# Latents as tokens x features from w_down to the output, the last MLP summed in PSUM, late adaLN units for latents alone, and weights split ahead

## The chip, the core and the metric

The kernel runs on one core of a Trainium2 chip. The metric is the device time of one execution in microseconds (us). In the profile the engines are PE (TensorE: PE for matmuls, PEld for the loads of their stationary operand), DVE (VectorE), ACT (ScalarE), POOL (GpSimd) and SP (SyncE, whose queue issues nearly all loads).

## The reference

256 latent tokens and 256 context tokens of 1024 features go through two layers. Layer 0 mixes tokens by a convolution, layer 1 by a bidirectional chunkwise mLSTM with 4 heads. Each mixer is followed by an MLP. The context leaves the computation within layer 1: only latents have an output.

```
sh1, sc1, g1, sh2, sc2, g2 = split(silu(c) @ ada_w[i] + ada_b[i], 6)      # per layer; c_ctx for the context
y = mixer(modulate(h, sh1, sc1))                                          # layer 1: ... @ w_down, 2048 -> 1024
h = layer_norm(ALPHA * h + g1 * y, ln1_g[i], ln1_b[i])
h = layer_norm(ALPHA * h + g2 * mlp(modulate(h, sh2, sc2)), ln2_g[i], ln2_b[i])
# mlp(u) = square(relu(u @ w1)) @ w2, 1024 -> 4096 -> 1024
# mLSTM output per head: y = (group_norm(o_f * h_f + o_b * h_b) * gn_g + skip * xc) * silu(z), then @ w_down
```

Everything is fp32. The mixer's layer 1 output of each head (512 features) is multiplied by that head's 512 rows of w_down, and the four products are summed.

## The kernel before

**Precision.** A product of two fp32 matrices is made of three fp32r matmuls: each operand is split into hi and lo, and hi·hi, hi·lo and lo·hi are summed in PSUM. `mm3` (L174 on; L177, L180, L181) has the weights as the stationary operand and up to 512 columns of tokens as the moving one, so its result is features x tokens. `mm3t` (L183; L185 to L187) has a block of 128 tokens as the stationary operand and 512 columns of weights as the moving one; its result is tokens x features. Weights come in 1 MB loads into `raw` (3 buffers, `raw_load`, L148) and are split in pieces of 1024 columns: a copy by ACT to `wh` and a subtraction by DVE to `wl` (4 buffers each, `split_w`, L160).

**Layout.** Nearly all activations lie as features x tokens. A layer norm (`Norm`, L428) over features is then a sum over partitions: PE sums columns with matmuls (`mean`, `col`), ACT squares, DVE sums the squares, and at the end (`finish`, L485) PE spreads the reciprocal roots over all partitions (L513), after which `apply` (L517) takes two DVE instructions for each of the 8 feature blocks.

**adaLN.** Layer 1 has 12 units of 512 columns of `ada_w`: 0 to 1 are sh1, 2 to 3 sc1, 4 to 5 g1, 6 to 7 sh2, 8 to 9 sc2, 10 to 11 g2. `AdaV` (L347) makes units 0 to 8 on DVE while PE works on something else: for each 128 rows one 256 KB load (`ar`), then a multiply-add each for the context and the latents into two accumulators `L`; PE sums the accumulators over partitions (L378), ACT copies, PE transposes (L387). Units 9, 10 and 11 are made by PE (`Ada`, L323, L297) inside the first norm of layer 1's end, as filling (`fill`, L1440), from six 1 MB loads.

**The end of layer 1**, where the change lies:
1. The attention stage follows the table `Z.att` (L46): main work (`o0` to `o3`: `gate_o`, output gates; then `D1 D2` and `D3`: `down`, products with w_down) and side work (`G` decay, `W` weights, `A` attend, `D0`) taken in turns.
2. `down` (L1398) makes, for each head and each of 8 feature blocks, 12 matmuls of 256 columns (`mm3`), and adds each result to the residual `hl` (features x tokens).
3. The join: the norm over `hl` with its filling, the modulation to `u` (L1456 to L1458), then the MLP.
4. `mlp` (L868) in four chunks of 1024 hidden features: 8 hidden blocks of 24 matmuls of 256 columns, their relu, square and split (`e1`), then 8 output blocks of 24 matmuls of 256 columns with w2, each added to `hl` by DVE (`e2`, L899).
5. The tail: the last norm, scale and offset by ACT (L1472), and 8 stores.

**Order.** A scheduler of the framework sets the order of instructions on each engine from its own estimates; every engine works through its queue in order. SP's queue is in order as well. PSUM has 8 banks under the tags mm (3), ln (2), cv (2) and fl (1).

## Time and profile before

| | |
|---|---|
| three runs | 1763.49, 1768.0, 1763.47 us; median 1763.49 us |
| the profiled execution | 1771.28 us, of which the span from the first to the last instruction 1769.6 us |
| matmuls | 10394 |
| DVE, ACT, POOL busy | 61%, 42%, 2% of the span |
| join: last matmul of w_down to the first of the last MLP | 1539.02 to 1562.76 us |
| last MLP, first to last matmul | 1562.76 to 1752.12 us |
| tail: end of the last MLP's matmuls to the end | 1752.12 to 1769.57 us |

Busy time is the time in which an engine has an instruction in progress. Matmuls overlap their neighbours, so the pace of a stretch is read from the count of matmuls in it, not from the length of one. Rows of groups read: line, engine, operation, output<-inputs, shapes, count | busy us, mean ns of one | idle time before it and what ended it. Rows of the timeline read: start, length (us), engine, line, operation, tiles, shapes, count, and in brackets idle time before it with what ended it.

### The profile page before, as it was taken

The numbers are of one execution on the slowest core, as the hardware profiler recorded it, in microseconds if no ns is written. First come the engines' busy times: TensorE is split into PE (matmuls) and PEld (weight loads), VectorE is DVE, ScalarE is ACT, GpSimd is POOL, SyncE is SP. The second block draws the span as 40 slices with busy tenths as digits, with TensorE's granted clock in tenths as the row PEclk, the third lists the DMA queues.
The fourth block names the chain that finished last, engine by engine and source line by source line (L and its number), as shares of the span: only waits on it lengthen the run. The fifth ranks groups of instructions, "written<-read, shape, count | busy, mean of one in ns | idle before, by whom it ended". The sixth has DMA issues, their size and how long they took to land.

```text
span 1769.6 us, 26027 instructions
## 1 busy us (share of the span) xinstructions
PE 1721.4 (97%) x10394; PEld 1452.6 (82%) x10394; DVE 1086.0 (61%) x1997; ACT 737.4 (42%) x1164; POOL 31.5 (2%) x84
## 2 busy tenths in 40 slices
PE   8999999999999999999999999999999999989996
PEld 5655798878788999976777998988777888879996
DVE  5456896566545787762234763633677766866666
ACT  3311663232324464542333433432577645434443
POOL 0000000000000000000000000000021000000000
PEclk9899999999999999999999999999999999989998
DMA  9333525344324075577745742533544555655551
GB/s 354 121 118 126 188 74 202 121 141 143 131 96 143 25 222 178 177 241 267 249 148 168 262 155 84 206 143 123 200 155 171 193 201 199 216 189 191 174 184 48
DMA packets 67817, 297.59 MB, mean 168 GB/s; under 512 B 6834, under 2 KB 22706, under 8 KB 36720
## 3 DMA queue, kind: packets, MB, share of 16 engines
q1 hardware_dynamic: 50032, 281.25, 45.3%
q10 hardware_dynamic: 17664, 14.69, 2.5%
q8 instruction: 82, 1.34, 0.3%
q14 instruction: 39, 0.32, 0.1%
HBM read 280.17 MB, written 15.73 MB: 167 GB/s over the span
## 4 chain that ended last, share of the span: by engine, by line
PE 91%; DVE 4%; ACT 2%; DMA 1%; issue 1%; SPq 0%; POOL 0%; POOLq 0%; ACTq 0%; DVEq 0%
PE mm L177 22%; PE mm L181 22%; PE mm L180 22%; PE mm L187 3%; PE mm L185 3%; PE mm L186 3%; PE fl L297 1%; DMA raw<-ada_w 1%; DVE wl L155 1%; PE cv L762 1%; PE fl L693 1%; PE ln L177 1%; PE ln L180 1%; PE ln L181 1%; PE cv L186 1%
## 5 line engine op out<-in xcount | busy, mean ns | idle before, releaser
L154 ACT CAST wh<-raw 128x1024 fp32r<-128x1024 f32 x354 | 367.9, 1048 | 606.1 <-PE mm L180 440.7
L155 DVE TENSOR_TENSOR wl<-raw,wh 128x1024 fp32r<-128x1024 f32 x354 | 431.8, 1224 | 298.7 <-ACT wh L154 296.5
L180 PE MATMUL mm<-u,wh 128*128 128x256 f32 (+1 forms) x1400 | 448.7, 321 | 0.0
L177 PE MATMUL mm<-u,wh 128*128 128x256 f32 (+1 forms) x1272 | 399.8, 315 | 7.4 <-ACT u L1456 2.1
L181 PE MATMUL mm<-u,wl 128*128 128x256 f32 (+1 forms) x1272 | 398.3, 314 | 1.1 <-DVE wl L155 1.1
L180 PEld LDWEIGHTS mm<-u,wh 128*128 128x128 f32 x1400 | 269.3, 192 | 18.9 <-DVE mv L528 0.8
L177 PEld LDWEIGHTS mm<-u,wh 128*128 128x128 f32 x1272 | 244.7, 193 | 29.9 <-ACT wh L154 7.4
L181 PEld LDWEIGHTS mm<-u,wl 128*128 128x128 f32 x1272 | 245.2, 193 | 16.7 <-DVE wl L155 2.3
L177 PE MATMUL mm<-hid,wh 128*128 128x256 f32 (+1 forms) x512 | 166.0, 324 | 0.0
L181 PE MATMUL mm<-hid,wl 128*128 128x256 f32 (+1 forms) x512 | 165.3, 323 | 0.0
L180 PE MATMUL mm<-hid,wh 128*128 128x256 f32 (+1 forms) x512 | 165.3, 323 | 0.0
L365 DVE SCALAR_TENSOR_TENSOR L<-ar,cs,L 128x512 f32<-128x512 f32 x126 | 90.0, 748 | 66.6 <-DMA ar<-ada_w 66.4
L177 PEld LDWEIGHTS mm<-hid,wh 128*128 128x128 f32 x512 | 97.4, 190 | 7.9 <-issue 0.2
L180 PEld LDWEIGHTS mm<-hid,wh 128*128 128x128 f32 x512 | 97.4, 190 | 7.7 <-issue 0.2
L181 PEld LDWEIGHTS mm<-hid,wl 128*128 128x128 f32 x512 | 97.4, 190 | 7.5
L177 PE MATMUL mm<-xm,wh 128*128 128x512 f32 x256 | 102.9, 402 | 0.0
L185 PE MATMUL mm<-wh,xl 128*128 128x512 f32 x256 | 101.0, 396 | 0.7 <-ACT wh L154 0.5
L186 PE MATMUL mm<-wh,xl 128*128 128x512 f32 x256 | 100.6, 393 | 0.6 <-DVE xl L155 0.6
L181 PE MATMUL mm<-xm,wl 128*128 128x512 f32 x256 | 100.3, 392 | 0.0
L187 PE MATMUL mm<-wl,xl 128*128 128x512 f32 x256 | 100.1, 394 | 0.2
L177 PE MATMUL mm<-qq,wh 128*128 128x272 f32 x256 | 74.1, 289 | 0.0
L181 PE MATMUL mm<-qq,wl 128*128 128x272 f32 x256 | 73.9, 289 | 0.0
(414 smaller groups left out, 2774.1 us busy)
## 6 DMA issues: line engine op xcount, KB each, us to landing
raw<-w SPq DMA_DIRECT2D x64, 1024.0 KB, 4.9
raw<-wo SPq DMA_DIRECT2D x32, 1024.0 KB, 4.9
raw<-ada_w SPq DMA_DIRECT2D x30, 1024.0 KB, 4.9
ar<-ada_w SPq DMA_DIRECT2D x72, 256.0 KB, 2.9
raw<-wv SPq DMA_DIRECT2D x16, 1024.0 KB, 6.0
raw<-wqT SPq DMA_DIRECT2D x16, 1024.0 KB, 5.3
raw<-wq SPq DMA_DIRECT2D x16, 1024.0 KB, 5.3
raw<-wk SPq DMA_DIRECT2D x16, 1024.0 KB, 4.8
```

What stands on the lines that cost most here:

```text
L154: c = nc.scalar.copy(hi, src)
L155: nc.vector.tensor_tensor(lo, src, hi.bitcast(F32), op=ALU.subtract)
L177: a = nc.tensor.matmul(ps, wh, xh, start=start, stop=False)
L180: nc.tensor.matmul(ps, wh, xl, start=False, stop=False)
L181: nc.tensor.matmul(ps, wl, xh, start=False, stop=stop)
L185: nc.tensor.matmul(ps, xh, wh, start=start, stop=False)
L186: nc.tensor.matmul(ps, xl, wh, start=False, stop=False)
L187: nc.tensor.matmul(ps, xh, wl, start=False, stop=stop)
L297: a = nc.tensor.matmul(ps[32 * j:32 * j + 32], cs[:, kt, 14 - 2 * v:46 - 2 * v], blocks[kt], start=first and kt < 4, stop=last and kt >= 4 ...
L365: nc.vector.scalar_tensor_tensor(a, w, c, a, op0=ALU.mult, op1=ALU.add)
L693: nc.tensor.matmul(wqs[0][32 * j:32 * j + 32, :], wgp[0][:, kt, :], raw[:, j * 512:(j + 1) * 512], start=kt == 0, stop=kt == ET - 1, tile_ ...
L762: return nc.tensor.matmul(o[r:r + 64, :], g_[:, r:r + 64], ps_[b][i], start=i == 0, stop=i == 1, tile_position=(0, r))
```

## The change

What it does, in the order of the program:

- **adaLN.** `AdaV` takes a list of units and of streams. Units 0 to 3 still have both streams, and four accumulators (two units) are now summed by four matmuls side by side. Units 6 to 9 (sh2, sc2) are made for latents alone, four accumulators at a time. Units 4 and 5 (g1), also for latents alone, are not brought to columns: a matmul with 128 columns of ones gives their sum on every partition as a row `G1` (two fp32 matmuls of 512 columns), to which the bias, loaded as a row on all partitions, is added. Units 10 and 11 (g2) are made by PE in the join; two matmuls (`gate2`) turn them into the row `G2`.
- **Residual.** After the up-projections' norm the latents are scaled by ACT and transposed by PE (16 transposes of 128x128) into `R`, tokens x features.
- **w_down** is laid out for `mm3t`: for each head 2 token blocks x 2 halves of 512 features, 12 matmuls of 512 columns each. Head 0 is added to `R` by DVE and POOL; heads 1 to 3 are summed in four PSUM banks (the three of mm and the one of fl). Head 3's weights are split ahead into buffers of their own (`E3`).
- **Join.** For each token block: the product with `G1`, the sum into `R` and BN_STATS on DVE, the root by ACT, two DVE instructions that normalise (512 columns each), 8 transposes on PE, and for each of the 8 feature blocks an ACT instruction (hi) and a DVE instruction, then a DVE subtraction for two blocks (lo). Two units of filling are left.
- **Last MLP.** w2 is laid out for `mm3t`; the sum over all four chunks stays in four PSUM banks (two of ln, two of cv). In the last chunk six of the eight weight pieces are held back so that token block 0 ends before block 1. While it runs POOL prepares the next residual in `R`.
- **Tail.** For each token block the norm as in the join; block 0's scale and offset by ACT and POOL, block 1's by four DVE instructions; four stores of 256 KB.
- `bo` is loaded in two parts for each head; `es` has one buffer where it had two.

The core of the diff:

```
-    att = [..., ['o3', 'A2', 1], ['D1 D2', 'A3', 1.2], ['D3', '', 0]]
+    att = [..., ['o3', 'A2', 1], ['D1 E3 D2', 'A3', 1.2], ['D3', '', 0]]
...
-    ada_g2, ada_n1, ada_n2 = Ada(0, 10, 2), AdaVs(1, 0, 4), AdaVs(1, 4, 8 - Z.fill)
+    ada_g2, ada_n1, ada_n2 = Ada(0, 10, 2), AdaV(1, range(4), (0, 1)), AdaV(1, range(6, 10), (1,), (4, 5))
...
+    R = xp.tile([P, 2, D], F32, name="res")
     for f in range(0, DT, 2):
+        t, tr = tmp("S"), psum("cv")
         for i in range(2):
+            nc.scalar.activation(t[:, i * C:(i + 1) * C], x[f + i][:, HI], AF.Identity, scale=..., bias=...)
+            for tt in range(2):
+                nc.tensor.transpose(tr[:, tt * C + i * P:...], t[:, i * C + tt * P:...], ident)
+        nc.scalar.copy(R[:, :, f * P:(f + 2) * P], tr.rearrange("p (t c) -> p t c", t=2))
...
-                for kt in range(4):
-                    mm3(ps, *kcol(w, (i % 2) * 4 + kt), *yy[h][kt], kt == 0, kt == 3)
-                nc.vector.scalar_tensor_tensor(hl[m], ps, g1[:, m:m + 1], hl[m], op0=ALU.mult, op1=ALU.add)
+        def mms(ps, ws, hf, t, first, last):
+            for kt in range(4):
+                mm3t(ps, yy[h][kt][0][:, BLK[t]], yy[h][kt][1][:, BLK[t]], *ws[hf][kt], first and kt == 0, last and kt == 3)
...
+    def residual(t, hf, ps, G):
+        e_ = tmp("E")
+        nc.vector.tensor_tensor(e_, ps, G[:, HF[hf]], op=ALU.mult)
+        nc.vector.tensor_tensor(R[:, t, HF[hf]], R[:, t, HF[hf]], e_, op=ALU.add)
+        nc.vector.bn_stats(nst[t][0][:, hf, :], R[:, t, HF[hf]])
+    def row_norm(t):
+        nc.vector.bn_aggr(mv[:, 0:2], ...)
+        nc.scalar.activation(mv[:, 2:3], mv[:, 1:2], AF.Sqrt, bias=eps)
+        nc.vector.reciprocal(mv[:, 2:3], mv[:, 2:3])
...
+    def ln1(t):
+        mv = row_norm(t)
+        for g_ in range(2):
+            nc.vector.tensor_scalar(R[:, t, HF[g_]], R[:, t, HF[g_]], mv[:, 0:1], mv[:, 2:3], op0=ALU.subtract, op1=ALU.mult)
+            tr = psum("ln")
+            for i in range(4):
+                nc.tensor.transpose(tr[:, i * P:(i + 1) * P], R[:, t, ...], ident)
+            for i in range(4):
+                nc.scalar.activation(UH[f // 2][:, f % 2, ts], tr[:, sl], AF.Identity, scale=ca[...], bias=cb[...])
+                nc.vector.tensor_scalar(y[:, sl], tr[:, sl], ca[...], cb[...], op0=ALU.mult, op1=ALU.add)
+                if i % 2:
+                    nc.vector.tensor_tensor(UL[f // 2][:, :, ts], y..., UH[f // 2].bitcast(F32)[:, :, ts], op=ALU.subtract)
...
+    for t in range(2):
+        for b_, op in ((GA, ALU.mult), (BA, ALU.add)):
+            nc.gpsimd.tensor_tensor(R[:, t, :], R[:, t, :], b_, op=op)
...
+        def w2_mm(w, kt, t, hf):
+            mm3t(acc[t][hf], hid[kt][0][:, ts], hid[kt][1][:, ts], w[0][hf], w[1][hf],
+                 c == 0 and kt == 0, c == 3 and kt == DT - 1)
```

**PE at the join.** Before, from the first filling after w_down's last matmul to the first matmuls of the last MLP: `fl<-raw,cs` is the filling, `ln<-inv_c` and `ln<-L,ones` the norm, `fl<-fold` the end of the filling, `mm<-u,wh` the MLP.

```order
L297 MATMUL fl_13941<-raw_13942,cs 32x512 x4
L297 MATMUL fl_13941<-raw_13944,cs 32x512 x4
L480 MATMUL ln_13954<-inv_c,x_11458 128x1 x2
L297 MATMUL fl_13941<-raw_13959,cs 32x512 x4
L480 MATMUL ln_13971<-inv_c,x_11459 128x1 x2
L297 MATMUL fl_13941<-raw_13961,cs 32x512 x4
L513 MATMUL ln_14006<-L_14004,ones 128x512
L297 MATMUL fl_13941<-raw_13984,cs 32x512 x4
L297 MATMUL fl_13941<-raw_13986,cs 32x512 x4
L305 MATMUL fl_13998<-fold,F_13996 128x6 x4
L177 MATMUL mm_14082<-u_14025,wh_13923 128x256
L177 MATMUL mm_14083<-u_14025,wh_13927 128x256
```

The same place now, from w_down's last matmul on: `ln<-ident,res` are the transposes (token block 0's two halves, then block 1's first half), `x_13686` the hi and `x_13690` the lo of the first two feature blocks. Block 1's second half stands 10 rows further, behind the first eight matmuls and the last filling.

```order
L186 MATMUL fl_13321<-xl_13477,og_13589 128x512
L1517 MATMUL ln_13698<-ident,res 128x128 x4
L1517 MATMUL ln_13715<-ident,res 128x128 x4
L296 MATMUL fl_13731<-raw_13732,cs 32x512 x4
L296 MATMUL fl_13731<-raw_13734,cs 32x512 x4
L296 MATMUL fl_13731<-raw_13744,cs 32x512 x4
L1517 MATMUL ln_13762<-ident,res 128x128 x4
L176 MATMUL mm_13815<-x_13686,wh_13663 128x256
L176 MATMUL mm_13816<-x_13686,wh_13667 128x256
L176 MATMUL mm_13817<-x_13686,wh_13673 128x256
L176 MATMUL cv_13818<-x_13686,wh_13677 128x256
L179 MATMUL mm_13815<-x_13690,wh_13663 128x256
```

Six loads of filling and the norm's column sums have become four loads and 16 transposes.

**DVE in the join, now**, from block 0's second normalisation on. `mv_13609` and `mv_13643` are the mean and root of blocks 0 and 1, `S<-ln` reads transposed features from PSUM, `x_13690` is the lo that the MLP's fifth matmul waits for. The brackets tell what an instruction waits for: `Activation_49` is a count that ACT raises, `DVE_49` one of DVE itself.

```order
L1514 TENSOR_SCALAR res<-res,mv_13609 128x512
L1480 BN_AGGR mv_13643<-st_13642 128x2 [waits DVE_49]
L1523 TENSOR_SCALAR S_13703<-ln_13698,ca_13681,cb_13682 128x128 [waits Activation_49]
L1482 RECIPROCAL mv_13643<-mv_13643 128x1 [waits Activation_49]
L1514 TENSOR_SCALAR res<-res,mv_13643 128x512 [waits DVE_49]
L1523 TENSOR_SCALAR S_13703<-ln_13698,ca_13681,cb_13682 128x128 [waits Activation_49]
L1514 TENSOR_SCALAR res<-res,mv_13643 128x512
L1526 TENSOR_TENSOR x_13690<-S_13703,x_13686 128x2x128 [waits DVE_49]
```

Both token blocks' work is mixed, and each of the 16 `S<-ln` waits for ACT; ACT's instructions on the same banks wait for DVE in the same way.

**DVE in the tail.** Before, from the squares' last sum to the first two instructions of `apply` (of 16):

```order
L473 TENSOR_TENSOR ln_14081<-ln_14081,L_16290 128x256
L482 TENSOR_SCALAR lc_16301<-ln_16298 128x2
L498 TENSOR_TENSOR lc_16301<-lc_16301,lc_16304 128x2
L501 RECIPROCAL lc_16308<-lc_16301 128x2
L502 SCALAR_TENSOR_TENSOR lc_16308<-lc_16296,lc_16308 128x2
L508 TENSOR_TENSOR L_16311<-ident,lc_16308 128x512
L519 TENSOR_TENSOR hl_5924<-hl_5924,ln_16313 128x256
L520 TENSOR_TENSOR hl_5924<-hl_5924,ln_16313 128x256
```

Now, from the product that reads the last PSUM bank to the end of DVE's queue (`row_13799` is G2, `row_13805` and `row_13807` are ln2's scale and offset):

```order
L1471 TENSOR_TENSOR E_15573<-cv_14094,row_13799 128x512
L1472 TENSOR_TENSOR res<-res,E_15573 128x512
L1475 BN_STATS st_15552<-res 128x6
L1480 BN_AGGR mv_15553<-st_15552 128x2
L1567 SCALAR_TENSOR_TENSOR E_15580<-res,mv_15553,row_13805 128x512
L1482 RECIPROCAL mv_15553<-mv_15553 128x1
L1567 SCALAR_TENSOR_TENSOR E_15581<-res,mv_15553,row_13805 128x512
L1570 SCALAR_TENSOR_TENSOR E_15580<-E_15580,mv_15553,row_13807 128x512
L1570 SCALAR_TENSOR_TENSOR E_15581<-E_15581,mv_15553,row_13807 128x512
```

PE's part in the tail and the 16 instructions of `apply` are gone; nine DVE instructions are left behind the last matmul.

More of the change, by code (lines that the diff above doesn't have):

```diff
@@ new lines, in sums, with end @@
+        def sums(self, accs):
+            ps = psum()
+            self.sb = tmp("F")
+            for i, a in enumerate(accs):
+                nc.tensor.matmul(ps[32 * i:32 * i + 32, :], ones[:, 0:32], a, start=True, stop=True,
+                                 tile_position=(0, 32 * i))
+            nc.scalar.copy(self.sb, ps)
+        def end(self, u):
+            ns, s0 = len(self.streams), self.streams[0]
+            nu, o = 4 // ns, _OFF[f"ada_b{self.l}"][0] + 4 * u
+            tr = psum()
@@ L404, in ad, with row @@
+                vecs[:, o:o + 4 * nu].rearrange("p (v b o) -> p b v o", b=4, o=1).broadcast_to([P, 4, nu, ns]), op=ALU.add)
+        def row(self, i, dst):
+            ps = psum()
+            nc.tensor.matmul(ps, ones, self.acc[i], start=True, stop=True)
+            nc.vector.tensor_tensor(dst, ps, dst, op=ALU.add)
     def ad(l, s, which):
@@ L928, in each1 @@
                 ada_g2.end()
-        if c in (1, 2):
+        if c in (1, 2) or (c == 3 and m < 2):
             ada_n1.step()
@@ L1392, in attend @@
             yield
[L1394 to L1413 removed]
+    pre1 = {}
@@ L1461, in after1 @@
[L1461 to L1473 removed]
+    HD, WX = maker(qf, "hid", 2 * DT), maker(qf, "wx", 8)
@@ new lines, in hybrid_kernel, with gate2 @@
+    G2, GA, BA, GN, BN = [rows(qf.tile([P, D], F32, name=f"row{i}"), rows_d[i:i + 1]) for i in range(1, 6)]
+    for b_ in (GA, BA):
+        nc.gpsimd.tensor_scalar(b_, b_, ALPHA, None, op0=ALU.mult)
+    for t in range(2):
+        for b_, op in ((GA, ALU.mult), (BA, ALU.add)):
+            nc.gpsimd.tensor_tensor(R[:, t, :], R[:, t, :], b_, op=op)
+    def gate2():
+        for v in range(2):
+            ps = psum()
+            nc.tensor.matmul(ps, fold[:, 2 * v + 1:2 * v + 2].broadcast_to([P, P]), ada_n3.sb, start=True, stop=True)
+            nc.vector.tensor_tensor(G2[:, HF[v]], ps, G2[:, HF[v]], op=ALU.add)
```

279 lines of the change are left out of this document (175 added, 104 removed).

## Prediction

> **What bounds the kernel now.** I read the first part of the page (busy time) and the chain first, then windows over stages, then the timeline at the two places where TensorE (PE) pauses.
>
> ```profile
> span 1769.6 us, 26027 instructions
> PE 1721.4 (97%) x10394; PEld 1452.6 (82%) x10394; DVE 1086.0 (61%) x1997; ACT 737.4 (42%) x1164; POOL 31.5 (2%) x84
> PE 91%; DVE 4%; ACT 2%; DMA 1%; issue 1%; SPq 0%; POOL 0%; POOLq 0%; ACTq 0%; DVEq 0%
> ```
>
> PE bounds nearly everywhere: 91% of the chain is PE, and only DVE, ACT and loads (7% together) stand in for it. A change gains here by fewer or cheaper matmuls, or where PE waits. What a matmul costs is read from windows in which PE never pauses (behind the length stand PE's busy time and count; the seventh number is the granted clock):
>
> ```profile
> 1444.20:1464.60 20.40, 20.40 (x91) 16.90 (x90) 9.91 (x12) 5.96 (x6) 0.00 (x0) 1.00 0.44 162
> 1600.00:1700.00 100.00, 100.00 (x836) 100.00 (x835) 63.05 (x86) 45.45 (x67) 0.00 (x0) 1.00 0.54 188
> 1444.22 0.39 PE L185 MATMUL cv<-wh,pw 128*128 128x512 f32 x1
> ```
>
> The first window holds only 512-column matmuls of the form of `mm3t`, 90 after the one that the edge cuts: 20.40/90 = 0.227 us each. The second lies in the last MLP: 835 of 256 columns, 0.120 us each. Two narrow ones cost 0.240, one wide 0.227.
>
> PE waits at the join and in the tail:
>
> ```profile
> 1539.02:1562.76 23.74, 14.66 (x70) 4.96 (x68) 16.91 (x52) 3.65 (x9) 0.00 (x0) 0.70 0.86 330
> 1562.76:1577.23 14.47, 14.47 (x96) 14.27 (x96) 7.36 (x24) 4.54 (x9) 0.00 (x0) 0.79 0.00 1
> ```
> ```profile
> 1539.02 0.28 PE L181 MATMUL mm<-og,wl 128*128 128x256 f32 x1
> 1545.24 1.94 PE L297 MATMUL fl<-raw,cs 128*32 128x512 f32 x8 [1.34 <-DMA raw<-ada_w]
> 1558.77 1.88 PE L305 MATMUL fl<-fold,F 128*128 128x6 f32 x8 [2.80 <-DVE F L337]
> 1562.76 1.01 PE L177 MATMUL mm<-u,wh 128*128 128x256 f32 x3 [2.11 <-ACT u L1456]
> ```
>
> The join lasts 23.74 us, filled with waits for loads, for the end of the filling and for the modulation. Behind it the granted clock is 0.79: 96 matmuls take 14.47 us, at full pace 96 x 0.120 = 11.5, so 2.9 more. The join costs 23.7 + 2.9 = 26.6. The tail:
>
> ```profile
> 1752.16 0.48 DVE L899 SCALAR_TENSOR_TENSOR hl<-mm,ada,hl 128x256 f32<-128x256 f32 x1 [0.50 <-PE mm L181]
> 1757.39 2.05 PE L513 MATMUL ln<-L,ones 128*128 128x512 f32 x2 [1.99 <-DVE L L508]
> 1766.25 0.60 ACT L1472 ACTIVATE E<-hl,vecs 128x256 f32<-128x256 f32 x1 [0.48 <-DVE hl L520]
> 1761.02 6.19 SPq L1473 DMA_DIRECT2D out<-E  x8
> ```
>
> From the last matmul (1752.12) to the end (1769.57) pass 17.45 us: sums, a spread of the roots by two fp32 matmuls (2.05), 16 DVE instructions, scale, stores.
>
> **The change part by part.**
>
> *Width.* w_down's 384 narrow matmuls become 192 wide ones, w2's 768 become 384: 576 x (0.240 - 0.227) = 7.5 us less, all on PE's path. The Trainium skill, "TensorE: Matmul & The Clock Gate", section Back-to-back issue gap, gives N/2.4 + 2.5 ns for an isolated matmul; by it a pair would save only 2.5 ns, an estimate of 1.4 us in all. The windows above are sustained and disagree with it, so 7.5 stands. The gain could turn into a loss only if something of a wide matmul is no longer hidden: that is rival B.
>
> *Norm and adaLN work on PE.*
>
> ```profile
> 1742.62 0.43 PE ln L452 x2
> 1743.05 0.34 PE ln L480 x4
> ```
> ```profile
> 1521.21 0.67 PE ln L1382 x6
> ```
> ```profile
> L378 PE MATMUL mm<-L,ones 128*32 128x512 f32 x36 | 9.5, 604 | 0.0
> ```
>
> The first pair stands within the last MLP (0.77 us) and has its like in w_down: 1.5 us go. The 36 sums of accumulators (9.5 us) become groups of four side by side; eight fillings of this form take 1.94 us in the join, so three groups of four take 2.9. G1 and G2 are two fp32 matmuls each, like the pair of L513 above that takes 2.05: 4.1. Twenty adaLN transposes become 12 and 16 for `R` come in: 8 more at 0.11, 0.9. Net 9.5 - 2.9 - 4.1 - 0.9 = 1.6 less; I take 0.9, since 604 ns is the time in progress and overlapped its neighbours. It can lie between 2 us more and, if G1's and G2's rows fall into waits of PE, 4.1 + 1.6 less. DVE's multiply-adds become fewer, as units 4 to 9 lose the context, and lie beside PE work as before (DVE 61% busy). The adaLN loads become 80 instead of 72 on SP's queue, 8 x 2.9 us of transfer in a stage in which PE does not wait; should a weight load behind them come late, PE waits up to its 4.9 us (row below).
>
> *The wait at D3.* Head 3's products need its y, made from its last attend matmul on by DVE, ACT and PE in turns:
>
> ```profile
> 1510.98 0.39 PE L187 MATMUL cv<-wl,pw 128*128 128x512 f32 x1
> 1524.17 0.68 DVE L155 TENSOR_TENSOR og<-og,og 128x512 fp32r<-128x512 f32 x1
> 1526.15 0.68 DVE L155 TENSOR_TENSOR og<-og,og 128x512 fp32r<-128x512 f32 x1
> ```
> ```profile
> L154 ACT CAST wh<-raw 128x1024 fp32r<-128x1024 f32 x354 | 367.9, 1048 | 606.1 <-PE mm L180 440.7
> L155 DVE TENSOR_TENSOR wl<-raw,wh 128x1024 fp32r<-128x1024 f32 x354 | 431.8, 1224 | 298.7 <-ACT wh L154 296.5
> ```
> ```profile
> raw<-ada_w SPq DMA_DIRECT2D x30, 1024.0 KB, 4.9
> ar<-ada_w SPq DMA_DIRECT2D x72, 256.0 KB, 2.9
> ```
>
> That chain took 1511.37 to 1524.85 for the first half, 13.5 us, and 15.5 for the second. D2, put behind it, covers 48 x 0.227 = 10.9 and the transposes about 0.9: PE will wait 1.7 to 3.7 unless DVE is freer than before: the additions to `hl` for each product of heads 1 to 3, which stood in its queue between the steps of y, are gone, and E3's splits come in. I take 1.2, between 0.5 and 3. Behind the waiting matmul stand the rest of D3 and the join, so all of it moves. E3 holds two of three `raw` buffers meanwhile; if one w_down load comes late, PE waits its 4.9 and a split's 1.05 + 1.22: 7.2. I count that at nothing, since D2's products give its loads 10.9 us of cover.
>
> *The join.* Its length is now DVE's queue from the last product of w_down to the last lo that the MLP's first group reads.
>
> ```profile
> L1340 DVE TENSOR_TENSOR og<-mm,bo 128x512 f32<-128x512 f32 x16 | 10.8, 682 | 0.9 <-PE mm L187 0.9
> L1364 DVE BATCH_NORM_STATS2 gst<-og 128x6 f32<-128x512 f32 x8 | 5.5, 689 | 0.1
> L1365 DVE BATCH_NORM_AGGREGATE gmv<-gst 128x2 f32<-128x6 f32 x8 | 1.4, 177 | 0.1
> L501 DVE RECIPROCAL lc<-lc 128x2 f32<-128x2 f32 x6 | 1.0, 161 | 1.1 <-ACT lc L499 1.1
> L781 DVE TENSOR_SCALAR u<-u,mv 128x512 f32<-128x512 f32 x8 | 4.0, 540 | 0.0
> L1281 DVE SCALAR_TENSOR_TENSOR S<-ln,acol,mask 128x128 f32<-128x128 f32 x8 | 2.7, 340 | 0.1
> ```
> ```profile
> L155 DVE TENSOR_TENSOR hid<-E,hid 128x256 fp32r<-128x256 f32 x32 | 13.5, 423 | 9.0 <-ACT hid L154 9.0
> L155 DVE TENSOR_TENSOR pw<-S,pw 128x256 fp32r<-128x256 f32 x21 | 11.8, 579 | 2.6 <-ACT pw L154 2.6
> ```
> ```profile
> L1283 ACT ACTIVATE S<-S 128x128 f32<-128x128 f32 x7 | 2.2, 307 | 0.5 <-DVE S L1281 0.5
> L499 ACT ACTIVATE lc<-lc,eps 128x2 f32<-128x2 f32 x2 | 0.6, 295 | 4.9 <-DVE lc L498 4.9
> ```
>
> Product 0.68, sum and statistics 0.69 each, aggregate 0.18, two reciprocals 0.33, four normalisations 2.16, nine reads of transposed features 3.06, four lo 1.68: 9.5 us. With 0.25 until the product starts and 1.3 for the hand-over between ACT (0.31 each) and DVE on each PSUM bank: 11.0. Then come the last filling of four matmuls (1.0, half of the 1.94 above), four transposes (0.5) and two last lo (0.8): 13.3; eight MLP matmuls are done on the way (1.0), so 12.3, and 2.7 for the lower clock, nearly the 2.9 of before since the pause is not much shorter (bounds 0 and 2.9): 15 against 26.6, 11.6 less. Bounds: 11, if the hand-overs overlap (1.3) and the clock stays (2.7); 20, if each of 16 hand-overs costs ACT's 0.31 in full (5.0). The fourth filling load waits for the first one's matmuls; its 4.9 lies beside the 11.0.
>
> *The tail.* Its new DVE form has its like in adaLN:
>
> ```profile
> L365 DVE SCALAR_TENSOR_TENSOR L<-ar,cs,L 128x512 f32<-128x512 f32 x126 | 90.0, 748 | 66.6 <-DMA ar<-ada_w 66.4
> ```
>
> Behind the last matmul: 0.04, product 0.68, sum 0.69, statistics 0.69, aggregate 0.18, four of scale and offset at 0.75, reciprocal 0.16, the root beside one of them: 5.4. The store of 256 KB as the load `ar`, 2.9: 8.3; POOL beside DVE makes it 9.0, by the 579 against 423 ns above (the `pw` subtractions run while POOL adds). 17.4 - 9.0 = 8.4 less. Block 0's four POOL instructions begin some 4 us before the last matmul; at 1.5 to 2.7 each (row under rival A) they end 2 to 6 us behind it, so their store ends between 5 and 9.5 us: hardly later than block 1's.
>
> Other edits at nothing: a piece of w2 takes 1.22 us of DVE and feeds 12 wide matmuls, 2.72 us of PE. `bo` in two loads: the second waits on SP for the first half's last reader, and weight loads stand behind it; the attention stage has two pieces of weights in hand at each time, and if that did not do, one load's 4.9 us comes out. One `es` buffer makes POOL's next sum wait for PE's reading of the last; POOL is 2% busy.
>
> Sum: 7.5 + 1.5 + 0.9 - 1.2 + 11.6 + 8.4 = 28.7, so 29 us less than the 1771.28 us of the profiled execution. The median of the runs is 1763.49, 7.8 lower; I take it that the difference is not in the stages that change, so the same 29 come off: 1734.5.
>
> **The rivals.**
>
> *A: POOL holds DVE.* POOL's product of block 0's residual starts when the transposes have read it, inside the join, and its two-input work reads the same memory as DVE's.
>
> ```profile
> L1295 POOL TENSOR_TENSOR es<-es,S 128x256 f32<-128x256 f32 x7 | 9.3, 1334 | 20.5 <-DVE S L1284 20.5
> ```
>
> 1024 columns take 4 x 1.33 = 5.3 us, two follow one another. If a DVE instruction waits for a whole one, the join is 5.3 to 10.6 longer and the tail 2.7 (512 columns): 8 to 13 us of the gain go, 1742.5 to 1747.5. The Trainium skill, "SBUF — State Buffer", section Who interferes with whom, calls the shared port an exclusive lock and so speaks for this. Against it: 579 ns is 0.16 us over 423, far under the 1.33 of a POOL instruction. Chance 0.15.
>
> *B, slower: exposed weight loads.* In w_down and w2 each 512-column matmul loads its own stationary operand.
>
> ```profile
> L177 PEld LDWEIGHTS mm<-hid,wh 128*128 128x128 f32 x512 | 97.4, 190 | 7.9 <-issue 0.2
> ```
>
> If these 0.19 us did not hide, 576 would cost 109 us: 1844. It would be slower by more than 0.3% (5.3 us, about what can be told from no change) once (29 + 5.3)/0.19 = 180 of 576 are exposed. Against it: in the window at 1444 each matmul has its own load and they hide. Chance 0.04.
>
> *C: no change.* Late w_down loads for four head halves, 7.2 us each because of the buffers that E3 holds, eat 29 us: 1763. Against it: the DMA share in that stage is about a half (0.44). Chance 0.03.
>
> **The numbers.** Forecast 0.78: 1734.5. Its own bounds: join 4 less, D3 0.7 less, tail 0.7 less, adaLN 4.8 less: 1724. The other way join 5, D3 1.8, adaLN 3, one late load 5 more: 1749, which holds A too (to 1747.5). The range 1724 to 1749 leaves out B, C and what has no name here. Faster 0.93 (forecast and A), same 0.03 (C), slower 0.04 (B).
>
> **What would show it.** Windows over w_down and the last MLP: 0.227 per 512-column matmul with no pause (else B). At D3's first matmul, idle time ended by DVE `y` of about 1 us. Join: the time from w_down's last matmul to the MLP's steady pace near 12.5, ended by DVE lo, and DVE's lo at 0.42, not over 2 us (else A); PE idle ended by a load there would make the join's sum wrong. Tail: 9 us, ended by the store of block 1 and not by POOL's block 0. If the join stays above 20, my count of DVE's queue is wrong.

## The result, and the profile after

The changed kernel takes 1735.43 us (median of 4 runs, 1733.79 to 1741.03) against 1763.95 for the kernel before: a ratio of 0.9846 (95% interval 0.9822 to 0.9870), 28.5 us less. A second set gave 1734.83 against 1763.48, ratio 0.9841 (0.9817 to 0.9866). The forecast was 1734.5. The total is right to 1 us, which is in part luck: the interval of the ratio leaves 23 to 31 us for the difference, and of the terms the join gave 2 us less than forecast while other stages together gave 1.3 us more in the profiles.

The page of the changed kernel, the same three lines as before:

```profile
span 1734.4 us, 24658 instructions
PE 1694.7 (98%) x9782; PEld 1415.4 (82%) x9782; DVE 1040.4 (60%) x1846; ACT 734.5 (42%) x1161; POOL 61.5 (4%) x98
PE 92%; DVE 4%; DMA 2%; ACT 1%; issue 1%; POOL 0%; SPq 0%; DVEq 0%; ACTq 0%; POOLq 0%
```

612 matmuls are gone and PE still bounds the kernel. POOL has twice the busy time it had. The windows of the changed kernel over a stretch of products with w2, over the join (from w_down's last matmul until the last MLP runs without a pause) and over the tail:

```profile
1572.00:1588.00 16.00, 16.00 (x72) 13.28 (x71) 7.35 (x6) 6.03 (x6) 0.00 (x0) 1.00 0.50 186
1526.31:1543.86 17.55, 10.54 (x56) 4.44 (x57) 13.21 (x29) 5.39 (x14) 10.34 (x4) 0.81 0.78 292
1725.40:1734.40 9.00, 0.00 (x0) 0.00 (x0) 5.76 (x9) 0.29 (x1) 1.49 (x2) 0.65 0.30 111
```

With w2 71 to 72 wide matmuls in 16 us: 0.225 us each, PE never pauses. The join is 17.55 us long, POOL works through 10.3 us of it. The tail is 9.00. What PE waited for, from 1509 us (the end of the attention stage) to 1535 us, and from the trace's timeline the steps of the join and of the tail that matter:

```profile
PE ln L1517 <- DVE res L1514: 2.3, 1, 2.3
PE mm L184 <- ACT og L153: 1.0, 1, 1.0
PE ln L1517 <- DVE mv L1480: 0.4, 1, 0.4
```
```profile
1530.34 4.32 PE L296 MATMUL fl<-raw,cs 128*32 128x512 f32 x24
1534.59 0.66 PE L1517 MATMUL ln<-ident,res 128*128 128x128 f32 x4
1536.39 2.34 POOL L1546 TENSOR_TENSOR res<-res,row 128x1024 f32<-128x1024 f32 x1
1536.56 2.45 DVE L1526 TENSOR_TENSOR x<-S,x 128x256 fp32r<-128x256 f32 x1
1540.24 0.55 PE L179 MATMUL mm<-x,wh 128*128 128x256 f32 x1 [3.72 <-DVE x L1526]
1541.37 1.94 PE L296 MATMUL fl<-raw,cs 128*32 128x512 f32 x8
```
```profile
1725.71 1.26 POOL L1563 TENSOR_TENSOR E<-E,row 128x512 f32<-128x512 f32 x1
1726.16 1.36 DVE L1472 TENSOR_TENSOR res<-res,E 128x512 f32<-128x512 f32 x1
1730.69 1.00 SPq L1571 DMA_DIRECT2D out<-E  x2
```

The wait of 1.0 us for `og` is the one at D3's start. In the join one lo, which DVE makes in 0.42 us elsewhere, took 2.45: it began 0.17 us after the start of POOL's multiplication of the residual and ended 0.28 us behind its end. It stood in DVE's queue ahead of the lo for which PE waited 3.72 us. In the tail DVE's last sum into the residual took 1.36 us instead of 0.69 and ended 0.55 us behind the end of a POOL instruction. In both cases DVE's instruction ends its usual length less 0.14 us behind POOL's end, as if it had got to work only then.

To compare joins I use two measures, both from w_down's last matmul on. The *start of the MLP* is the time at which its matmuls begin to follow one another without a pause or another instruction, less 0.12 us for each of them done before: 23.5 us before, 16.6 after (16.2 in the second profile of the changed kernel). The *effective join* is the start of the last MLP's 180th matmul less 179 x 0.1198 us, so that a lowered clock behind the join counts as well: 27.5 us before, 18.0 after (17.5). Of it 1.2 us are in both kernels pauses from the 96th matmul on, which the prediction's 26.6 and 15 did not hold; up to the 96th it is 26.3 and 16.7. The two profiled executions, stage by stage:

| stage | before, us | after, us | difference | forecast |
|---|---|---|---|---|
| start to the first matmul with `hid` as moving operand (same matmuls in both) | 297.0 | 289.8 | -7.2 | 0 |
| from there to the end of w_down | 1242.3 | 1236.5 | -5.8 | -5.0 |
| effective join | 27.51 | 17.95 | -9.6 | -11.6 |
| rest of the last MLP (first 179 matmuls at full pace in both) | 185.3 | 181.1 | -4.2 | -3.7 |
| tail | 17.45 | 9.00 | -8.4 | -8.4 |

The forecast column sorts the prediction's terms by stage. The first row is not a term of the change. PE's work there is the same, at another granted clock (the seventh number); the kernel before first, the changed one behind it:

```profile
0.00:297.00 297.00, 281.14 (x1625) 203.68 (x1626) 195.82 (x502) 117.99 (x220) 4.78 (x24) 0.97 0.46 170
```
```profile
0.00:289.80 289.80, 274.68 (x1624) 200.64 (x1625) 191.32 (x492) 117.95 (x218) 4.77 (x24) 0.99 0.46 172
```

0.97 x 297.0 = 288.1 and 0.99 x 289.8 = 286.9: at full clock the two are nearly equal. These 7.2 us are of the size of the 7.8 us by which the profiled execution of before lay over its median. The profiles differ by 35.2 us, the medians by 28.5; the prediction's step of taking the same 29 us off the median stood on the assumption that the difference lies in stages that do not change, and these two profiles bear it out.

The second row holds two losses of the changed kernel for which the prediction has no term: in layer 1's up-projections PE waits once for 2.5 us (1.4 before) for DVE to read a PSUM bank, and just behind it the clock is at a half for 3.4 us, 1.7 us of time, where the kernel before has no such stretch:

```profile
618.70:622.11 3.41, 3.41 (x16) 3.41 (x17) 3.28 (x10) 2.01 (x4) 0.00 (x0) 0.50 0.35 115
```

### The profile page after: what moved, and what is told of

The parts are those of the page before. It is cut to its first block, busy times and chain, and to the rows that moved or that the text cites. A ratio compares the mean times of both kernels' runs of the same rounds, so it can differ in the third digit from the quotient of the medians.

```text
span 1734.4 us, 24658 instructions
## 1 busy us (share of the span) xinstructions
PE 1694.7 (98%) x9782; PEld 1415.4 (82%) x9782; DVE 1040.4 (60%) x1846; ACT 734.5 (42%) x1161; POOL 61.5 (4%) x98
## 4 chain that ended last, share of the span: by engine, by line
PE 92%; DVE 4%; DMA 2%; ACT 1%; issue 1%; POOL 0%; SPq 0%; DVEq 0%; ACTq 0%; POOLq 0%
PE mm L176 21%; PE mm L180 20%; PE mm L179 20%; PE mm L184 3%; PE mm L185 3%; PE mm L186 3%; PE fl L296 2%; PE cv L186 2%; PE cv L185 2%; PE cv L184 2%; PE fl L697 1%; PE cv L766 1%; DMA raw<-ada_w 1%; PE ln L185 1%; PE ln L184 1%
## 5 line engine op out<-in xcount | busy, mean ns | idle before, releaser
L179 PE MATMUL mm<-u,wh 128*128 128x256 f32 (+1 forms) x1152 | 377.3, 328 | 0.0
L176 PE MATMUL mm<-u,wh 128*128 128x256 f32 (+1 forms) x1024 | 328.2, 322 | 6.1 <-DVE E L982 2.5
L180 PE MATMUL mm<-u,wl 128*128 128x256 f32 (+1 forms) x1024 | 326.7, 320 | 0.0
L179 PEld LDWEIGHTS mm<-u,wh 128*128 128x128 f32 x1152 | 220.6, 192 | 18.4 <-DVE mv L532 0.8
L176 PEld LDWEIGHTS mm<-u,wh 128*128 128x128 f32 x1024 | 196.1, 192 | 28.7 <-ACT wh L153 6.5
L180 PEld LDWEIGHTS mm<-u,wl 128*128 128x128 f32 x1024 | 196.4, 192 | 16.1 <-DVE wl L154 1.7
L179 PE MATMUL mm<-x,wh 128*128 128x256 f32 (+1 forms) x376 | 120.4, 320 | 3.7 <-DVE x L1526 3.7
L176 PE MATMUL mm<-hid,wh 128*128 128x512 f32 (+1 forms) x256 | 93.3, 365 | 0.0
L180 PE MATMUL mm<-hid,wl 128*128 128x512 f32 (+1 forms) x256 | 92.8, 363 | 0.0
L179 PE MATMUL mm<-hid,wh 128*128 128x512 f32 (+1 forms) x256 | 92.8, 363 | 0.0
L372 DVE SCALAR_TENSOR_TENSOR S<-ar,cs,S 128x512 f32<-128x512 f32 x56 | 40.8, 749 | 70.0 <-DMA ar<-ada_w 69.9
L179 PEld LDWEIGHTS mm<-x,wh 128*128 128x128 f32 x376 | 71.8, 191 | 9.3 <-DVE x L1526 3.9
L179 PE MATMUL mm<-qq,wh 128*128 128x272 f32 x256 | 73.9, 289 | 0.0
L176 PE MATMUL mm<-qq,wh 128*128 128x272 f32 x256 | 73.9, 288 | 0.0
```

The source lines that it names most:

```text
L176: a = nc.tensor.matmul(ps, wh, xh, start=start, stop=False)
L179: nc.tensor.matmul(ps, wh, xl, start=False, stop=False)
L180: nc.tensor.matmul(ps, wl, xh, start=False, stop=stop)
L372: nc.vector.scalar_tensor_tensor(a, w, c, a, op0=ALU.mult, op1=ALU.add)
```

## The experiments

All but the last two are single executions with a profile, from 1729.5 us (more_cover_for_d3) to 1747.8 us (no_weights_ahead). Their total moves by some us with the clock of the early stages, so the trace decides. The joins, in us from w_down's last matmul on:

| kernel | first lo matmul | start of the MLP | last lo starts | effective join |
|---|---|---|---|---|
| changed kernel, two profiles | 13.9, 13.6 | 16.6, 16.2 | 21.9, 21.6 | 18.0, 17.5 |
| w2_narrow (join as the changed kernel) | 12.1 | 15.0 | 21.3 | 17.4 |
| late_residual | 11.7 | 14.2 | 19.3 | 16.4 |
| no_filling | 12.4 | 13.4 | 19.0 | 16.0 |
| no_filling_late_residual | 10.9 | 11.9 | 17.4 | 13.9 |
| pool_pieces | 11.4 | 14.7 | 19.8 | 16.4 |
| grouped_turns | 13.1 | 12.6 | 15.6 | 14.0 |
| grouped_turns_free_filling | 13.1 | 12.6 | 17.5 | 14.1 |
| tail_on_dve (join as grouped_turns) | 13.7 | 13.2 | 16.2 | 16.1 |
| more_cover_for_d3 (same) | 12.7 | 12.2 | 15.2 | 13.6 |
| all_four (same) | 12.9 | 12.4 | 15.3 | 14.6 |

The last three and grouped_turns have one join, and the effective join differs by up to 2.5 us among them: the clock falls to a half for 3.4 us at a time, at other points in each execution. The windows of the same 19 us in grouped_turns and in tail_on_dve show it, at 0.91 and 0.82:

```profile
1525.11:1544.11 19.00, 14.37 (x101) 9.33 (x102) 13.13 (x36) 6.21 (x18) 0.00 (x0) 0.91 0.86 318
```
```profile
1528.65:1547.65 19.00, 13.68 (x84) 8.69 (x84) 13.14 (x36) 6.21 (x18) 0.00 (x0) 0.82 0.82 309
```

The start of the MLP moves by 1.0 us among the four. It moves by 1.6 us among the three executions of the changed kernel's join: in w2_narrow, whose MLP starts first, the clock falls to a half only 11.5 us behind w_down, and the three fillings ahead of block 1's transposes take 2.78 us in place of 4.32. A gain below 1.6 us is therefore read only between executions in which the half clock falls at the same places.

**late_residual.** POOL's preparation of the residual is moved out of the join.

```
-    for b_ in (GA, BA):
-        nc.gpsimd.tensor_scalar(b_, b_, ALPHA, None, op0=ALU.mult)
-    ...                                    # and the two-input instructions on R
     ...                                    # in the last MLP, chunk 0, behind e1
+    nc.vector.tensor_scalar(al2, hid[0][0]...[:, 0:1], 0.0, ALPHA, op0=ALU.mult, op1=ALU.add)
+    for b_ in (GA, BA):
+        nc.gpsimd.tensor_scalar(b_, b_, al2, None, op0=ALU.mult)
+    ...                                    # and the two-input instructions on R, unchanged
```

> POOL's preparation of the residual is made to wait for the first hidden block of the last MLP; nothing else moves, PE's order is the same. In the changed kernel one lo of the join took 2.45 us while POOL multiplied (0.42 alone), and from w_down's last matmul to the MLP's steady pace 17.5 us passed. Theory 1 (a DVE instruction with two SBUF inputs waits for the whole of a POOL instruction with two): every lo of the join takes about 0.42 and the pace is reached 2.0 us sooner, 15.5 us. Theory 2 (the hold is hidden, since PE waits for the last filling and block 1's transposes anyway): the lo shrink, but the pace comes at most 0.5 us sooner, 17 us or more.

The eight lo of the changed kernel, and then of late_residual:

```profile
L1526 DVE TENSOR_TENSOR x<-S,x 128x256 fp32r<-128x256 f32 x8 | 6.9, 864 | 0.2
```
```profile
L1526 DVE TENSOR_TENSOR x<-S,x 128x256 fp32r<-128x256 f32 x8 | 3.4, 422 | 0.2
```

Every lo is back at 0.42 us. The first lo matmul starts 1.9 to 2.2 us sooner than in the two profiles of the changed kernel and the MLP 2.0 to 2.4, as theory 1 said. In these three executions the half clock falls at the same places (it sets in 3.2 to 3.8 and 13.5 to 14.0 us behind w_down), so the gain is not the clock's. The effective join is only 1.1 to 1.5 us shorter, since a part of the second lowered stretch now falls behind the MLP's start. Theory 2 (0.5 at most) is out.

**no_filling.** The two calls of `ada_n3.mm()` are replaced by zeros.

> Leaves out the filling of the join (units 10 and 11 of adaLN; G2 then holds the bias alone). Theory 1 (PE works through its queue in order, so 3 of 4 filling loads stand in front of block 1's transposes and the fourth in front of the MLP's pace): the join of 17.5 us loses about 1.3 us before block 1's transposes and 1.9 us behind the first lo, to 14.5 us or less. Theory 2 (the join is set by ACT and DVE taking turns on the PSUM banks of the transposes, the filling only uses PE's idle time): 17 us.

The MLP starts 2.8 to 3.2 us sooner, as theory 1 said (in its own measure, up to the last pause of PE, 14.7 us against 14.5 or less); the effective join (16.0) shows only 1.5 to 2.0 of it, again by the clock, which is at a half from 3.8 to 17.5 us behind w_down. PE's waits from 1500 to 1570 us show what came in place (the first three rows):

```profile
PE ln L1517 <- DVE S L1523: 2.9, 1, 2.9
PE mm L179 <- DVE x L1526: 2.5, 1, 2.5
PE ln L1517 <- DVE res L1514: 2.3, 1, 2.3
```

Without the filling, block 1's transposes wait 2.9 us for DVE to read the PSUM bank that they reuse. Most of the filling's 4.3 us in front of them had lain in that wait: these transposes start 1.3 us sooner (7.0 instead of 8.3 us after w_down), no more.

**no_filling_late_residual.** Both edits.

> Both edits of the two kernels before: no filling (units 10 and 11 left out) and POOL's preparation behind the first hidden block. Theory 1: both gains add up, 17.5 - 3.2 - 2.0, about 12.3 us, which is the length that the prediction's count of DVE's queue gave. Theory 2 (turns on the PSUM banks set it): 16 us or more.

The MLP starts after 11.9 us, 4.3 to 4.7 sooner than in the changed kernel; the two gains alone sum to 4.8 to 5.6, so they add up but for 0.5 to 0.9 us. In theory 1's own measure, up to the last pause of PE, it is 13.2 us and not 12.3, still far from theory 2's 16 (the effective join, with the clock's part and the pauses behind the 96th matmul, is 13.9). The first lo matmul starts after 10.9 us; the prediction's count of DVE's queue up to there was 11.0.

**pool_pieces.** POOL's two-input instructions in pieces of 128 columns (0.49 us each).

```
-            nc.gpsimd.tensor_tensor(R[:, t, :], R[:, t, :], b_, op=op)
+            for q in range(8):
+                nc.gpsimd.tensor_tensor(R[:, t, qs], R[:, t, qs], b_[:, qs], op=op)   # qs: 128 columns
     ...                                    # and in the tail 4 pieces of each 512 columns
```

> POOL's two-input instructions on the residual and in the tail are cut into pieces of 128 columns (8 and 4 pieces), the data and the order stay. Theory 1 (DVE waits for the end of the POOL instruction that runs): a wait is now at most one piece, some 0.4 us, so no lo of the join takes over 0.9 us and the last sum into the residual (1.36 us in the tail) at most 1.1 us; join about 16 us. Theory 2 (DVE and POOL share the bandwidth as long as both work): the same total is lost, a lo of 2 us or several of 1 us in the join, and 1.3 us in the tail.

DVE's lo and its last sum in the tail of pool_pieces:

```profile
L1526 DVE TENSOR_TENSOR x<-S,x 128x256 fp32r<-128x256 f32 x8 | 4.5, 567 | 0.2
1730.39 0.85 DVE L1472 TENSOR_TENSOR res<-res,E 128x512 f32<-128x512 f32 x1
```

DVE's excess over 8 x 0.42 falls from 3.5 to 1.1 us, and in the tail from 0.67 to 0.16, though POOL works longer (14.6 us instead of 9.6). Theory 1: the wait is for the running instruction, not for a share of bandwidth. One lo still took 1.08 us, over the 0.9 expected: it ran beside POOL's `TENSOR_SCALAR` of 1024 columns, which was not cut. The tail as a whole got no shorter (9.05 us): the 16 pieces keep POOL at work for 8.6 us, and behind the sum they lengthen DVE's scale and offset by 0.33.

**grouped_turns.** late_residual, and for each half block ACT's four instructions first, then DVE's:

```
             for i in range(4):
                 nc.scalar.activation(UH[f // 2][:, f % 2, ts], tr[:, sl], ...)
+            for i in range(4):
+                f, sl = ...
                 nc.vector.tensor_scalar(y[:, sl], tr[:, sl], ...)
```

> POOL's preparation late as in late_residual, and for each half block ACT's four hi come first, then DVE's four reads (in the changed kernel they alternate on one PSUM bank, about 0.95 us for each pair, and only one bank is read at a time). The effective join (start of the 180th matmul of the MLP less 179 x 0.1198 us, from w_down's last matmul on) was 17.95 us in the changed kernel, 16.4 in late_residual, 13.9 with neither filling nor POOL. Theory 3 (the turns are what is left of the join): DVE reads one bank while ACT reads the other, the first lo matmul starts before 10 us instead of 11.7, effective join 14.5 us or less. Rival (DVE's own work or the filling sets it): 16.0 to 16.6 us.

The MLP starts 1.6 us sooner than in late_residual, the last lo 3.7. The effective join of 14.0 is within theory 3's bound (14.5), but it does not settle the matter: tail_on_dve, with the same join, has 16.1, which is the rival's range. There the half clock sets in at 3.6 and 13.8 us, as in late_residual (3.6 and 13.8), and the windows of the same 19 us agree (this one is late_residual's, tail_on_dve's stands above):

```profile
1525.81:1544.81 19.00, 13.56 (x81) 8.19 (x82) 13.38 (x35) 7.22 (x18) 0.00 (x0) 0.82 0.86 304
```

With the clock alike the MLP starts 0.9 us sooner, and 0.3 of that is left in the effective join. More than that is not shown to come from the regrouping. ACT's four hi of one bank now take 1.51 us in one piece:

```profile
1528.10 1.51 ACT L1521 ACTIVATE x<-ln,cb,ca 128x128 fp32r<-128x128 f32 x4 [2.87 <-PE ln L1517]
1529.63 1.05 DVE L1525 TENSOR_SCALAR S<-ln,ca,cb 128x128 f32<-128x128 f32 x3 [1.19 <-ACT x L1521]
1529.67 1.51 ACT L1521 ACTIVATE x<-ln,cb,ca 128x128 fp32r<-128x128 f32 x4
```

While DVE reads the first bank, ACT reads the second; in the changed kernel each pair of one hi and one read took 0.95 us on one bank. But theory 3's way is wrong: the first lo matmul did not come before 10 us, but at 13.1, later than in late_residual. The first pair of features is ready no sooner (its lo ends after 12.3 us); what comes sooner is all that follows, block 1's second transposes above all (10.1 instead of 14.3 us after w_down), so that PE does them while it waits. Then the fourth filling, which waits 1.3 us for its load, stands in front of the first lo matmul.

**grouped_turns_free_filling.** Filling behind both blocks in the program and not pinned.

> As grouped_turns, and the filling is written behind both blocks and not pinned, so that PE may take a part of it in the 2.3 us in which it waits for block 0's normalisation. Theory (each wait of the join has its own cause, and filling in front of transposes is one): effective join about 12.5 us. Rival (the filling's loads are not there so early, and the filling now stands in front of block 0's transposes): no better than grouped_turns, or up to 2 us worse.

No better than grouped_turns (12.6 and 14.1 us); the rival holds. PE's waits from 1500 to 1570 us, the filling in front:

```profile
PE fl L296 <- DMA raw<-ada_w: 2.1, 1, 2.1
PE mm L184 <- ACT og L153: 1.0, 1, 1.0
PE fl L296 <- DVE E L1471: 1.0, 1, 1.0
```

The filling does use the time ahead of block 0's transposes, but then has to wait 2.1 us for its last load in front of the MLP.

**w2_narrow.** Each product with w2 as two matmuls of 256 columns.

```
-            mm3t(acc[t][hf], hid[kt][0][:, ts], hid[kt][1][:, ts], w[0][hf], w[1][hf], ...)
+            for sl in ([slice(0, T)] if first or last_ else [LO, HI]):
+                mm3t(acc[t][hf][:, sl], hid[kt][0][:, ts], hid[kt][1][:, ts], w[0][hf][:, sl], w[1][hf][:, sl], ...)
```

> The changed kernel, with the products with w2 made as two matmuls of 256 columns in place of one of 512 (all but those of the first and the last of 32 pieces). The prediction's term says 13 ns for each pair: 360 pairs, 4.7 us more. By the formula for an isolated matmul 2.5 ns, 0.9 us. If the second load of the same stationary operand were not hidden, 0.19 us each, 68 us.

From the MLP's 180th matmul to its last 164.46 us pass instead of 159.69: 4.77 more. The same 16 us as above:

```profile
1572.00:1588.00 16.00, 16.00 (x136) 16.00 (x135) 7.35 (x6) 5.34 (x6) 0.00 (x0) 1.00 0.49 175
```

The prediction's 13 ns for a pair stand (4.7 us expected). The 2.5 ns that follow from the formula in the Trainium skill, "TensorE: Matmul & The Clock Gate", section Back-to-back issue gap (an estimate of 0.9 us), do not.

**no_weights_ahead.** `att` with `['D1 D2', 'A3', 1.2], ['E3 D3', '', 0]`.

> Head 3's weights are loaded and split behind D2 and no longer between D1 and D2. In the changed kernel PE waits 1.04 us at D3, for y. Theory (y is what is late, and weights could be loaded in time either way): the wait stays 1.0 to 1.5 us, no change in time. Rival (splitting ahead is what keeps the wait short): at least a split more, 2.3 us, or a load and a split, 7.2 us.

PE's waits:

```profile
PE ln L1517 <- DVE res L1514: 4.4, 1, 4.4
PE mm L184 <- ACT og L153: 3.5, 1, 3.5
PE ln L1401 <- ACT og L1393: 1.5, 2, 1.2
```

The wait at D3 grows from 1.0 to 3.5 us, 2.4 more, as the rival said (2.3 at least), but not for its reason. From the end of the last attend matmul to D3's first matmul pass 11.7 us, in the changed kernel 13.0: y is not later behind attend, it is sooner. What is missing is cover. In the changed kernel 48 matmuls of D2 stand in between, here 24, 5.4 us less. The table takes 1.2 steps of attend behind each step of the main work. `E3` is two more such steps in front of D2, so that with it attend ends ahead of all of D2. So the edit moves attend as well as the weights, and what the place of the splits costs by itself this run does not show.

The wait ahead of block 0's transposes grows by 2.1, and from the attention stage's first product with v to w_down's end 229.6 us pass instead of 223.5, 6.1 more. Of these, 2.4 are the longer wait and 1.5 the waits ahead of y's transposes. Nearly all of the rest is the clock: behind the wait it is at a half until 1528.89, 4.36 us in which PE never pauses, 2.2 us of time.

```profile
1524.53:1528.89 4.36, 4.36 (x10) 3.50 (x11) 3.61 (x5) 1.50 (x3) 0.00 (x0) 0.50 0.80 265
```

**tail_on_dve.** grouped_turns, with `if False:` for `if t == 0:` in `finish`, so that both blocks take DVE's branch.

> grouped_turns, and token block 0's scale and offset at the end are made by DVE as block 1's are, so POOL does nothing in the tail. Theory 1 (in the tail DVE's last sum into the residual waited for POOL, 1.36 us in place of 0.69, and DVE has time for block 0 in its two pauses before the last matmul): that sum takes 0.69 us and the tail falls from 9.0 to 8.3 us. Rival (DVE is the bound of the tail, and block 0's four instructions of 0.75 us push block 1's back): the tail grows, up to 12 us.

```profile
1726.64 0.69 DVE L1472 TENSOR_TENSOR res<-res,E 128x512 f32<-128x512 f32 x1
1725.90:1734.20 8.30, 0.00 (x0) 0.00 (x0) 5.08 (x9) 0.29 (x1) 0.00 (x0) 0.76 0.16 63
```

Theory 1: the sum takes 0.69 us, the tail 8.3.

**more_cover_for_d3.** `['D1 E3 D2', 'A3', 2]`.

> grouped_turns, with attend of head 3 taken in at a faster rate beside D1, E3 and D2 (2 steps for each in place of 1.2), so that it ends sooner and more of D2's products are left to cover y. Theory (y is what is late at D3): the wait of 1.04 us goes, w_down ends about 1 us sooner. Rival (attend's own inputs, or the splits of weights, are then late instead): PE waits as long or longer at another place, 0 to 3 us slower.

PE's waits from 1500 to 1530 us, all of them:

```profile
PE ln L1517 <- DVE res L1514: 2.2, 1, 2.2
PE ln L1517 <- DVE mv L1480: 0.4, 1, 0.4
```

The wait at D3 is gone, and w_down ends 1.0 us sooner (1524.09 against 1525.11 in grouped_turns). Head 3's weights are split at the same place in the table; only attend ends sooner.

**all_four and changed_again.** late_residual, grouped_turns, tail_on_dve and more_cover_for_d3 together, and the changed kernel beside it, five rounds each.

> The four correct edits that each took a wait away, together: POOL's preparation late, grouped turns, the tail on DVE, more cover for D3. If each wait had its own place, their gains add up in the trace: effective join 17.95 to 13.6 us (4.4), tail 9.0 to 8.3 (0.7), D3 1.0: 6.1 us less than the changed kernel, about 1729 us. If a gain is given back elsewhere (the slack of one is used up by another), less than 4 us.

> The changed kernel unaltered, on the same chip as all_four, for the difference of the two: 1735 us, 6 us over all_four if the gains add up, under 4 us if not. Its ratio to the kernel before should be about 0.984 again.

1732.68 us (1729.06 to 1739.41), ratio 0.9829 (0.9804 to 0.9854), against 1734.83 (1732.23 to 1741.42), ratio 0.9841 (0.9817 to 0.9866). The two intervals overlap: that all_four is faster than the changed kernel is not shown by the times. By the profiles the spans are 1729.6 and 1734.3, 4.7 us less, of which the join 2.9, the tail 0.7 and D3 about 1 (0.2 of its wait is left):

```profile
PE ln L1517 <- DVE res L1514: 2.7, 2, 2.2
PE fl L296 <- DMA raw<-ada_w: 1.3, 1, 1.3
PE mm L176 <- ACT x L1521: 0.5, 1, 0.5
...
PE mm L184 <- ACT og L153: 0.2, 1, 0.2
```

Under the 6.1 expected and over the 4 of the other case. The difference to 6.1 is the join (14.6 instead of 13.6, against 17.5 instead of 18.0), of the size by which the clock alone moves it.

## Why the prediction was right, and where it was not

- **Width, 7.5 us.** Right. 0.225 us in the window, and 4.77 us for 360 pairs against 4.7. Rival B (exposed weight loads) is out: PE never pauses in that window.
- **Norm, adaLN, width of w_down, up to w_down's end, 5.0 us less with D3's wait.** 5.8 measured, net of the two losses in the up-projections (1.1 of wait, 1.7 of clock), which the prediction does not have. Without them it is 8.6: the terms are undersized by some 3.6 us, and that the stage came out near 5.0 is luck. One part is seen: PE's waits ahead of adaLN's transposes (2.8 us in three waits before, 0.8 in one now), to which the prediction gave nothing. The 4.1 for G1 and G2 is right (1.9 us each), but by two errors that cancel: the row of 2.05 us was one matmul in two records, not a pair, and it ran at the half clock (0.50 from 1757.39 to 1759.44). The rest, and whether the longer wait belongs to the change, was not tried.
- **D3, 1.2 us.** 1.04, ended by `og`, as the prediction said. y took 13.0 us from the last attend matmul on (13.5 assumed), and the 48 matmuls of D2 covered the rest. That cover is what no_weights_ahead halves and more_cover_for_d3 lengthens; the prediction looked for the risk of E3 in the buffers that it holds, and what the table did with attend was more. Rival C's late loads did not come.
- **The tail, 8.4 us.** Right, in the sum and in the part for POOL: 0.7 forecast (8.3 to 9.0), 0.67 measured, and 8.3 without POOL in tail_on_dve. But the reason was wrong. I took it for a slowdown shared by all two-input instructions; it was one instruction that waited for POOL's to end.
- **The join, 11.6 us.** 9.6 measured (26.3 to 16.7, against 26.6 to 15). The count of DVE's queue was right: 11.0 us until the first group's lo, 10.9 with neither POOL nor filling in the way. What failed is the step "A: POOL holds DVE" against the forecast, as if only one of the two could be: the hold came in the forecast's own course, at 2.2 us. By the prediction's own sign (a lo over 2 us, else A) A came, at a fraction of the 8 to 13 us that it was priced at.

  I had set it aside by the mean of 579 against 423 ns. That mean is of two kinds: without POOL beside it a subtraction of `pw` with 256 columns took 0.41 to 0.43 us, and five of those that began while POOL worked took 0.95 to 0.97. The profile of the kernel before shows the hold in both directions:

```profile
1417.25 1.84 POOL L1295 TENSOR_TENSOR es<-es,S 128x256 f32<-128x256 f32 x1 [2.23 <-DVE S L1284]
1417.29 1.21 DVE L155 TENSOR_TENSOR wl<-raw,wh 128x1024 fp32r<-128x1024 f32 x1
1418.42 0.95 DVE L155 TENSOR_TENSOR pw<-S,pw 128x256 fp32r<-128x256 f32 x1
```

  POOL's instruction, 0.74 us where nothing holds it, lasts beyond the end of DVE's split, and the subtraction behind the split ends 0.28 us behind POOL, the same 0.28 as in the join. For the same reason A's price was too high: the 1.33 us for 256 columns is a mean of 0.74 and of 1.59 to 1.85 for held ones, and POOL's 1024 columns take 2.4 us and not 5.3; and one long hold fell in front of PE, not two.

  Next, "the last filling of four matmuls (1.0)" took 1.94 and the transposes behind it 0.87, not 0.5, at the half clock. The 1.94 that the prediction halved was already one whole filling (its four matmuls are eight records), and at the half clock (0.50 from 1545.24 to 1547.18 in the kernel before); at full clock one takes 1.07 us, in grouped_turns. The "two last lo (0.8)" did not come, PE goes on without a pause; in their place four matmuls between the first lo and the filling took 1.13 at the half clock. The three fillings in front of block 1's transposes cost 0.9.

  Against that the 2.7 us "for the lower clock" behind the join came to about 0.1: the lowered stretches fell inside the join (0.81 in its window). In sum 2.2 + 0.9 + 1.3 - 2.6 = 1.8, for 1.7 by which the 15 was exceeded (1.3 is what passed between the first lo matmul and the MLP's pace beyond the 2.3 forecast). ACT's and DVE's turns cost what the prediction gave them up to the first lo; behind it, where it counted nothing, regrouping gained 0.9 us at a like clock.
- **The sum.** The join gave 2 us less than forecast, the two stages beside it 1.3 more, and these errors offset one another. By the medians 28.5 stand against 28.7; by the profiles, without the first row of the table, 28.0.

The Trainium skill's "SBUF — State Buffer", section Who interferes with whom, says that a DVE instruction with two SBUF inputs contends with a POOL instruction that reads SBUF, and calls the shared port an exclusive lock. For POOL's `TENSOR_TENSOR` the runs agree, to the end of the instruction: the lo of 2.45 us ended 0.28 us behind it, and cutting it shortened the hold. With its `TENSOR_SCALAR`, which reads SBUF too, the hold ended well before the instruction, as in the second profile of the changed kernel:

```profile
1533.54 2.77 POOL L1543 TENSOR_SCALAR row<-row 128x1024 f32<-128x1024 f32 x1 [110.07 <-ACT x L1521]
1533.64 1.22 DVE L1526 TENSOR_TENSOR x<-S,x 128x256 fp32r<-128x256 f32 x1
```

The lo ended 1.32 us after POOL's start, 1.45 before its end.

## What to carry to other kernels

Before work is given to POOL because it is idle, look which DVE instruction with two SBUF inputs will stand in front of PE at that time, and move the POOL work behind it. Cutting it in pieces bounds each hold (here it shortened the join and not the tail). A mean over a stage hides that hold; single rows of the timeline, DVE's and POOL's side by side, show it. A change of a schedule's table can move more than the piece that it names: count the cover of a wait before and after. A count of one engine's queue gives the length of a join only up to the first instruction that PE needs; what PE itself has queued behind it (filling, transposes, in order) is counted at the clock that PE has there. Work that fills a wait costs only what is gained by leaving it out: here 3 us of 6 us of filling.

## What the runs showed of the hardware

- The granted clock falls to a half in stretches of 3.4 us or multiples (0.50 from 618.70 to 622.11 in the changed kernel), and where they fall differs between executions of one join: 0.91 and 0.82 over the same 19 us, with 2.1 us between the effective joins.
- A stretch of 290 us with the same matmuls took 7.2 us more at a mean granted clock of 0.97 than at 0.99: the difference between these two profiles is for a good part made there.
- POOL's two-input instruction takes 0.49 us for 128 columns, 0.74 for 256, 1.3 for 512 and 2.4 for 1024, and up to 1.85 for 256 where a 1024-column subtraction of DVE ran beside it.
